# A hybrid encoder layer: 42 instead of 32 of 256 tokens served by gathered expert rows

## The chip, the cores and the metric

The kernel runs on one core of a Trainium2 chip. The metric is the device time of one execution in microseconds, the median of three runs. The core has a matrix engine (PE, with its weight loads listed apart as PEld), a vector engine (DVE), an activation engine (ACT), GpSimd (POOL), a queue engine that only issues transfers (SP), and 16 DMA engines.

## The reference

One encoder layer over 256 tokens of width 2048: a combined input projection, windowed attention, a state-space branch, a gated merge, and then PEER, in which the change lies. Cut to that part:

```
def peer(h, w_query, sub_keys_1, sub_keys_2, expert_down, expert_up):
    q = (ht @ w_query).reshape(t_, PEER_HEADS, 2, PEER_HALF)
    s1 = einsum('thd,hkd->thk', q[:, :, 0], sub_keys_1)
    s2 = einsum('thd,hkd->thk', q[:, :, 1], sub_keys_2)
    v1, i1 = top_k(s1, 16);  v2, i2 = top_k(s2, 16)
    ...
    top_s, pos = top_k(cand, 16)             # 8 heads x 16 = 128 experts for each token
    gate = softmax(top_s)
    ...
    u_sel = take(expert_down, ib)            # 16384 experts of width 2048
    act = einsum('tkd,td->tk', u_sel, hb)
    w = gb * gelu(act)
    v_sel = take(expert_up, ib)
    return einsum('tk,tkd->td', w, v_sel)
```

## The kernel before, in words

Up to the query projection of PEER the layer works through dense products; that part is not touched. For PEER the 256 tokens are divided. The first `NGT` = 32 tokens have their 128 expert rows fetched one by one from memory (**gathered**). The other `ND` = 224 tokens are computed **densely**: every one of the 16,384 experts is multiplied with every one of the 224 tokens, and a gate matrix (zero where an expert was not chosen) selects.

**The down stage** (lines 1299 to 1335) has 256 steps. A step takes half of a chunk of 128 experts: a 512 KB block `raw` is loaded on SP's queue into one of four buffers, ACT rounds it to `whi`, DVE subtracts the two to `wlo` (two buffers each), and PE issues 8 *high* products (line 1324: `whi` against the high and the low part of the tokens side by side, 2 x 224 = 448 columns) and 8 *low* ones (line 1331: `wlo` against the high part, 224 columns). After every second step `add` and `gelu` make the chunk's activations. **The up stage** (lines 1384 to 1464) has twice 128 steps (h = 0 and 1) of the same make: `raw`, `whi`, `wlo`, then 8 high products with the activations `wt` (high and low part, 448 columns, line 1415) and 8 low ones (224 columns, line 1418). For h = 1 two of the eight outputs are kept in a shared bank, and their high product is issued as two of 224 columns (lines 1412 and 1413).

Beside the steps run pieces of other work, put in by credits: at each step `pump` and `pump_bg` add a budget to a counter, and a generator is advanced until the counter is used up. Each `yield` names the cost of the piece before it, and `yield None` ends the pump's turn at this step. The order of each engine's instructions is fixed by this when the program is built (`pin`).

- `route` (line 1035), paced by `RB` = 1.2 a step: the sixteen best keys and experts for each head, mostly on DVE. It starts with the down stage. Its first piece, `scores`, goes through PE and ACT over some steps, and the first `top8` on DVE needs its result `sS`.
- `gates` (line 1129), paced by `GB` = 1.12, follows `route`: for four tokens at a time DVE makes one-hot rows `oh`, PE multiplies them (line 1154), and DVE or ACT puts the result `ax` into the activations `A0` and `A1` (`onto`).
- `gather` (line 1173), in the background queue `bg`, paced by `HB` = 0.42 a step in the down stage and `UB` = 0.55 in the up stage: `SG` = 4 slots of 32 tokens stand side by side on `PU` = 128 partitions, so that one indirect transfer on POOL's queue brings half rows (4 KB) of 128 experts, and `NGG` = 32 groups times two halves cover the 128 experts of each token. 64 times DVE forms a product and its sum (line 1219, cost 1.25) for the down table; then come a gelu and 64 times a scaled addition (line 146, into `last`, cost 1.2) for the up table. The up rows can start only when the down stage is over. `fold` then adds the slots up.
- `flips` (line 1371), after `gather` in the same queue: transposes and writes the first half of the output during h = 1.

Of the kernel before, what the change touches and what calls it, by code (L numbers as in the profile page):

```python
# [17 lines left out]
OP = mybir.AluOpType  # L18
AX = mybir.AxisListType

P = 128
# [22 lines left out]
GB = 1.12  # L44


NGT = 32
SG = 4
NGG = -(-128 // SG)
PU = SG * NGT  # L50
ND = T - NGT
HB = 0.42
LAND = 4
UB = 0.55


def _prep(x, mix_norm_g, w_in, q_norm_g, k_norm_g, attn_sink, w_attn_o,
# [54 lines left out]
def _layer(ctx: ExitStack, tc: tile.TileContext, a, out):  # L112
# [20 lines left out]
    def ax_ps():  # L133
        return psx.tile([P, 512], F32, name="ax", tag="ax")

    def tt(o, i0, i1, op, eng=None):
        return (eng or V).tensor_tensor(o, i0, i1, op=op)  # L137

    def ts(o, i0, s1, op0, s2=None, op1=None, eng=None):
        if op1 is None:  # L140
            (eng or V).tensor_scalar(o, i0, s1, None, op0=op0)  # L141
        else:
            (eng or V).tensor_scalar(o, i0, s1, s2, op0=op0, op1=op1)

    def stt(o, i0, s, i1, op0, op1, **kw):
        V.scalar_tensor_tensor(o, i0, s, i1, op0=op0, op1=op1, **kw)  # L146
# [4 lines left out]
    def copy(o, i, **kw):  # L151
        S.activation(o, i, AF.Copy, **kw)  # L152

    def f32(ap):
        return ap.bitcast(F32)
# [30 lines left out]
    for i2 in range(2):  # L186
        for q in range(2):
            p0 = i2 * 64 + q * 32
# [753 lines left out]
    iota = rt.tile([P, P], F32, name="iota")  # L942
# [6 lines left out]
    picks = rt.tile([P, 3, T], F32, name="picks")  # L949
# [14 lines left out]
    def top8(src, val, idx, scr=None):  # L964
        V.max(val, src)
        V.max_index(idx, val, src)
        if scr is not None:
            V.match_replace(out=scr, in_to_replace=val, in_values=src, imm_value=NEG)
# [21 lines left out]
    def slots():  # L990

        fl = rp.tile([P, 2, SG * NGG], F32, name="slf")
        ix = rp.tile([P, 2, SG * NGG], I32, name="sli")
        V.memset(fl, 0.0)
        tn = slice(0, NGT)
        stt(fl[tn, 0, 0:P], sel[0][tn, 0, :], float(NK), sel[0][tn, 1, :], OP.mult, OP.add)
        V.tensor_copy(fl[tn, 1, 0:P], sel[0][tn, 2, :])
        for h in range(2):
            ts(ix[tn, h], fl[tn, 0], 2.0, OP.mult, float(h), OP.add)
        for s_ in range(SG):  # L1000
            ps, gs = slice(s_ * NGT, (s_ + 1) * NGT), slice(s_ * NGG, (s_ + 1) * NGG)
            nc.gpsimd.dma_start(rix[ps], ix[tn, :, gs])
# [24 lines left out]
    state = {"half": 0}  # L1027

    def onward(gen):

        if moved[0] == state["half"]:
            yield None
        moved[0] = state["half"]
        next(gen, None)

    def route():
        items = [(b, cc) for b in range(NB) for cc in range(4)]
        first = scores(*items[0])
        while not scored:
            yield from onward(first)  # L1040
        for n, (b, cc) in enumerate(items):
            ahead = scores(*items[n + 1]) if n + 1 < len(items) else iter(())
            sS = scored.pop(0)
            val = rp.tile([P, 4, TOPK], F32, name="val", tag="val", bufs=2)
            idx = rp.tile([P, 4, TOPK], U32, name="idx", tag="idx", bufs=2)
            scr = rp.tile([P, P], F32, name="scr", tag="scr", bufs=2)
            for j in range(4):
                top8(sS[:, j, :], val[:, j, 0:8], idx[:, j, 0:8], scr)
                top8(scr, val[:, j, 8:16], idx[:, j, 8:16])
                yield 1.2  # L1050
                yield from onward(ahead)
            idf = rp.tile([P, 4, TOPK], F32, name="idf", tag="idf", bufs=2)
            V.tensor_copy(idf, idx)
            tops = rp.tile([P, 2, TOPK], F32, name="tops", tag="tops", bufs=2)
            pos = rp.tile([P, 2, TOPK], U32, name="pos", tag="pos", bufs=2)
            cand = rp.tile([P, TOPK, TOPK], F32, name="cand", tag="cand", bufs=2)
            cnd2 = rp.tile([P, TOPK * TOPK], F32, name="cnd2", tag="cnd2", bufs=2)
            for h in range(2):
                tt(cand, val[:, 2 * h, :].unsqueeze(2).to_broadcast([P, TOPK, TOPK]),
                   val[:, 2 * h + 1, :].unsqueeze(1).to_broadcast([P, TOPK, TOPK]), OP.add)  # L1060
                top8(cand.rearrange("p a b -> p (a b)"), tops[:, h, 0:8], pos[:, h, 0:8], cnd2)
                yield 1.5
                top8(cnd2, tops[:, h, 8:16], pos[:, h, 8:16])
                yield 0.75
            h0 = cc * 2 * TOPK
            gv = sel[b][:, 2, h0:h0 + 2 * TOPK].rearrange("p (h k) -> p h k", h=2)
            tt(gv, tops, tops[:, :, 0:1].to_broadcast([P, 2, TOPK]), OP.subtract)
            ab = rp.tile([P, 2, 2, TOPK], U32, name="ab", tag="ab", bufs=2)
            abf = rp.tile([P, 2, 2, TOPK], F32, name="abf", tag="abf", bufs=2)
            ts(ab[:, 0], pos, 4, OP.logical_shift_right)  # L1070
            ts(ab[:, 1], pos, 15, OP.bitwise_and)
            V.tensor_copy(abf.rearrange("p a h k -> p (a h k)"), ab.rearrange("p a h k -> p (a h k)"))
            yield 0.4
            eq = rp.tile([P, 2 * TOPK, TOPK], F32, name="eq", tag="eq", bufs=2)
            for w in range(2):
                tt(eq, abf[:, w].rearrange("p h k -> p (h k)").unsqueeze(2).to_broadcast(
                    [P, 2 * TOPK, TOPK]), iota16.unsqueeze(1).to_broadcast([P, 2 * TOPK, TOPK]),
                   OP.is_equal)
                for h in range(2):
                    e_ = eq[:, h * TOPK:(h + 1) * TOPK, :]  # L1080
                    tt(e_, e_, idf[:, 2 * h + w, :].unsqueeze(1).to_broadcast([P, TOPK, TOPK]), OP.mult)
                yield 1.25
                V.tensor_reduce(sel[b][:, w, h0:h0 + 2 * TOPK], eq, axis=AX.X, op=OP.add)
                yield 0.6
            while len(scored) == 0 and n + 1 < len(items):
                yield from onward(ahead)
            if cc == 3:
                yield from finish(b)
# [4 lines left out]
    def scaled():  # L1093
# [8 lines left out]
        for k in range(KD):  # L1102
            hs = rp.tile([P, ND], F32, name="hs", tag="hs", bufs=2)
            tt(hs, f32(xsh[:, k, NGT:]), f32(xsl[:, k, NGT:]), OP.add)
            tt(hs, hs, R[:, NGT:], OP.mult)
            copy(h2[:, k, 0, :], hs)
# [22 lines left out]
    def gates():  # L1129

        made, summed = [], []

        def onto():
            p0, gp = summed.pop(0)
            gv = gp.rearrange("p (t c) -> p t c", t=4)
            n = state["chunk"]
            for tile_, base, nch in ((A0, 0, CA), (A1, CA, NK - CA)):
                m = min(max(n - base, 0), nch)
                av = tile_[:, :, p0:p0 + 4].rearrange("p c t -> p t c")
                if m > 0:  # L1140
                    tt(av[:, :, :m], av[:, :, :m], gv[:, :, base:base + m], OP.mult)
                if m < nch:
                    copy(av[:, :, m:], gv[:, :, base + m:base + nch])
            state["tok"] = p0 + 4

        for t0 in range(0, ND + 8, 4):
            if summed:
                onto()
                yield 1.3
            if made:  # L1150
                p0, oh = made.pop(0)
                gp = ax_ps()
                for j in range(4):
                    PE.matmul(gp[:, j * P:(j + 1) * P], lhsT=oh[:, 0, j], rhs=oh[:, 1, j],
                              start=True, stop=True)
                summed.append((p0, gp))
            if t0 < ND:
                oh = rt.tile([P, 2, 4, P], F32, name="oh", tag="oh", bufs=2)
                tk = slice(NGT + t0, NGT + t0 + 4)
                tt(oh, iota.unsqueeze(1).unsqueeze(1).to_broadcast([P, 2, 4, P]),  # L1160
                   picks[:, 0:2, tk].unsqueeze(3).to_broadcast([P, 2, 4, P]), OP.is_equal)
                yield 1.15
                tt(oh[:, 1], oh[:, 1], picks[:, 2, tk].unsqueeze(2).to_broadcast([P, 4, P]), OP.mult)
                made.append((t0, oh))
                yield 0.6
            else:
                yield None

# [3 lines left out]
    def gather():  # L1172
# [6 lines left out]

        for s_ in range(SG):  # L1180
            ps = slice(s_ * NGT, (s_ + 1) * NGT)
# [119 lines left out]
    for s_ in range(2 * NK):  # L1301
        c, q = divmod(s_, 2)
# [9 lines left out]
        pump(RB if A1 is None else GB)  # L1312
        pump_bg(HB)
        nxt.append(next(ready))
# [67 lines left out]
    for h in range(2):  # L1382
# [11 lines left out]
        for c in range(NK):  # L1394
# [4 lines left out]
            if more:  # L1399
                nxt = [next(ready)]  # L1400
                gate_high((c + 1) % NK)
            pump_bg(UB)
            if more:
# [64 lines left out]
```

## Time and profile before

| | |
|---|---|
| median of 3 runs | 2305.19 us (2304.98 to 2305.86) |
| the profiled execution, its own time | 2304.5 us |
| its span, first to last instruction | 2302.7 us |
| busy, PE | 2238.8 us (97%) |
| busy, DVE | 1831.2 us (80%) |
| busy, ACT | 1217.9 us (53%) |
| mean DMA rate over the span | 225 GB/s |
| down stage | from 909.6 us to 1635 us |
| up stage | from 1637.7 us to the end |

The profile shows one execution. Busy times are per engine and overlap; a busy engine far from the end of a chain costs nothing. The times of the program's stages are those of the first and the last of their instructions in the timeline.

### The profile page before, as it was taken

How to read it: one execution, taken by the hardware profiler on the slowest of the kernel's cores; microseconds unless marked ns; L12 is line 12 of the kernel's file. 1: busy time of each engine (PE TensorE's matmuls, PEld its weight loads, DVE VectorE, ACT ScalarE, POOL GpSimd, SP SyncE). 2: the span in 40 equal slices, each digit the busy share in tenths (PEclk: the TensorE clock that was granted, in tenths of full speed). 3: DMA queues.
4: the chain of work that ended last, by engine and by line, in shares of the span. 5: the costliest groups of instructions: out<-in, count | busy, mean ns of one | idle time of the engine just before them, and what ended most of it. 6: DMA issues, size and time to landing. Idle time of an engine off the chain costs nothing. (4 is left out here: it accounts for less than half of the span.)

```text
span 2302.7 us, 36932 instructions
## 1 busy us (share of the span) xinstructions
PE 2238.8 (97%) x13298; PEld 1995.9 (87%) x13298; DVE 1831.2 (80%) x3819; ACT 1217.9 (53%) x2090; POOL 314.2 (14%) x309
## 2 busy tenths in 40 slices
PE   8999899999999999999999999999999999999999
PEld 6788676678888888898989999999999999999998
DVE  7858999974566565999989999999778878875565
ACT  5885654334344554455555555555555555554554
POOL 3320000001000100000012222112223322210000
PEclk9999999999999999999999999999999999999999
DMA  7854345566666765565577777777889888876664
GB/s 240 269 181 137 128 135 167 175 220 200 220 208 201 239 214 190 170 195 184 194 247 256 250 240 247 249 247 246 293 292 320 303 307 307 294 254 229 204 209 156
DMA packets 145464, 519.03 MB, mean 225 GB/s; under 512 B 18032, under 2 KB 18656, under 8 KB 144896
## 3 DMA queue, kind: packets, MB, share of 16 engines
q1 hardware_dynamic: 113184, 410.04, 53.2%
q0 software_dynamic: 30944, 105.56, 13.1%
q8 instruction: 104, 1.70, 0.3%
q10 hardware_dynamic: 1152, 1.07, 0.1%
q14 instruction: 80, 0.66, 0.1%
HBM read 496.11 MB, written 18.87 MB: 224 GB/s over the span
## 5 line engine op out<-in xcount | busy, mean ns | idle before, releaser
L152 ACT ACTIVATE whi<-raw 128x1024 fp32r<-128x1024 f32 x768 | 814.5, 1061 | 929.5 <-PE mm L286 227.5
L137 DVE TENSOR_TENSOR wlo<-raw,whi 128x1024 fp32r<-128x1024 f32 x768 | 939.1, 1223 | 389.9 <-ACT whi L152 372.7
L1324 PE MATMUL mm<-h,whi 128*128 128x448 f32 x2048 | 479.4, 370 | 0.1
L1324 PEld LDWEIGHTS mm<-h,whi 128*128 128x128 f32 x2048 | 367.3, 189 | 23.2 <-ACT whi L152 0.6
L1331 PEld LDWEIGHTS mm<-h,wlo 128*128 128x128 f32 x2048 | 265.9, 191 | 25.6 <-DVE wlo L137 18.5
L1331 PE MATMUL mm<-h,wlo 128*128 128x224 f32 x2048 | 271.3, 275 | 9.2 <-DVE wlo L137 8.6
L1415 PE MATMUL mm<-wt,whi 128*128 128x448 f32 x1024 | 252.2, 367 | 3.7 <-DVE wt L137 3.7
L285 PE MATMUL mm<-whi,hb 128*128 128x512 f32 x512 | 204.2, 401 | 7.7 <-DVE hb L141 6.4
L286 PE MATMUL mm<-whi,hb 128*128 128x512 f32 x512 | 202.8, 398 | 0.3 <-DVE hb L146 0.2
L1415 PE MATMUL ax<-wt,whi 128*128 128x448 f32 x768 | 198.1, 365 | 0.0
L1415 PEld LDWEIGHTS mm<-wt,whi 128*128 128x128 f32 x1024 | 174.5, 190 | 14.9 <-issue 3.3
L1204 POOL DMA_INDIRECT rows<-in_down_rows_dram,rix x64 | 108.8, 1700 | 394.5 <-DVE dots L1219 378.0
L289 PE MATMUL mm<-wlo,hb 128*128 128x512 f32 x512 | 148.3, 407 | 10.2 <-DVE wlo L137 10.0
L1418 PE MATMUL ax<-wt,wlo 128*128 128x224 f32 x1024 | 156.8, 275 | 0.0
L1418 PE MATMUL mm<-wt,wlo 128*128 128x224 f32 x1024 | 156.5, 275 | 0.0
L1415 PEld LDWEIGHTS ax<-wt,whi 128*128 128x128 f32 x768 | 144.1, 188 | 10.3
L1418 PEld LDWEIGHTS mm<-wt,wlo 128*128 128x128 f32 x1024 | 144.9, 191 | 3.9
L1418 PEld LDWEIGHTS ax<-wt,wlo 128*128 128x128 f32 x1024 | 135.8, 193 | 0.0
L289 PEld LDWEIGHTS mm<-wlo,hb 128*128 128x128 f32 x512 | 92.9, 189 | 44.4 <-DVE wlo L137 26.4
L285 PEld LDWEIGHTS mm<-whi,hb 128*128 128x128 f32 x512 | 97.0, 190 | 30.2 <-ACT whi L152 10.2
L286 PEld LDWEIGHTS mm<-whi,hb 128*128 128x128 f32 x512 | 96.9, 190 | 20.1 <-DVE hb L146 1.1
L137 DVE TENSOR_TENSOR X<-X,s 128x64 f32<-128x64 f32 x508 | 107.9, 282 | 0.0
(276 smaller groups left out, 3190.2 us busy)
## 6 DMA issues: line engine op xcount, KB each, us to landing
raw<-in_down_dram SPq DMA_DIRECT2D x256, 512.0 KB, 4.2
raw<-in_up_dram SPq DMA_DIRECT2D x256, 512.0 KB, 4.8
raw<-in_w_in_dram SPq DMA_DIRECT2D x128, 512.0 KB, 3.6
raw<-in_w_ao_dram SPq DMA_DIRECT2D x32, 512.0 KB, 3.9
raw<-in_w_out_dram SPq DMA_DIRECT2D x32, 512.0 KB, 4.0
raw<-in_w_q_dram SPq DMA_DIRECT2D x32, 512.0 KB, 4.5
raw<-in_wgb_dram SPq DMA_DIRECT2D x16, 512.0 KB, 4.4
raw<-in_wga_dram SPq DMA_DIRECT2D x16, 512.0 KB, 3.7
```

What stands on the lines that cost most here:

```text
L137: return (eng or V).tensor_tensor(o, i0, i1, op=op)
L152: S.activation(o, i, AF.Copy, **kw)
L285: PE.matmul(ps[b], lhsT=lh[:, k, bs], rhs=h_, start=(k == 0), stop=False)
L286: PE.matmul(ps[b], lhsT=ll[:, k, bs], rhs=h_, start=False, stop=False)
L289: PE.matmul(ps[b], lhsT=lh[:, k, b * P:(b + 1) * P], rhs=lo[:, j * 512:(j + 1) * 512], start=False, stop=(k == 2 * nu - 1))
L1204: nc.gpsimd.indirect_dma_start(out=r[:PU], out_offset=None, in_=table, in_offset=bass.IndirectOffsetOnAxis(ap=rix[:PU, h, g:g + 1], axis=0))
L1324: PE.matmul(ps[:, :2 * ND], lhsT=hi[:, j * P:(j + 1) * P], rhs=h2[:, k].rearrange("p a t -> p (a t)"), start=(k == 0), stop=(k == KD - 1), ...
L1331: PE.matmul(ps[:, :ND], lhsT=lo[:, j * P:(j + 1) * P], rhs=h2[:, q * 8 + j, 0, :], start=False, stop=False, skip_group_check=True)
L1415: PE.matmul(acc[i][:, :2 * ND], lhsT=w_, rhs=wv, start=first, stop=False, skip_group_check=True)
L1418: PE.matmul(region(i)[0], lhsT=lo[:, i * P:(i + 1) * P], rhs=wh, start=False, stop=end, skip_group_check=True)
```

## The change

Three constants say how many tokens are gathered: 42 in three slots (126 partitions, 43 groups of experts, 86 transfers for each table) in place of 32 in four; 214 tokens remain dense. The background's pace is 0.40 a step in the down stage and 0.66 in the up stage. `route` gives up two further turns between its first scores and the first `top8`; `gates` gives up one after its first one-hot rows, and takes a last group of two tokens, since 214 is not a multiple of four.

```
-NGT = 32
-SG = 4
+NGT = 42
+SG = 3
 NGG = -(-128 // SG)
 PU = SG * NGT
 ND = T - NGT
-HB = 0.42
+HB = 0.4
 LAND = 4
-UB = 0.55
+UB = 0.66
...
         while not scored:
             yield from onward(first)
+        yield None
+        yield None
...
         for t0 in range(0, ND + 8, 4):
             if summed:
                 onto()
                 yield 1.3
             if made:
-                p0, oh = made.pop(0)
+                p0, nt, oh = made.pop(0)
                 gp = ax_ps()
-                for j in range(4):
+                for j in range(nt):
                     PE.matmul(gp[:, j * P:(j + 1) * P], lhsT=oh[:, 0, j], rhs=oh[:, 1, j],
                               start=True, stop=True)
-                summed.append((p0, gp))
+                summed.append((p0, nt, gp))
             if t0 < ND:
+                nt = min(4, ND - t0)
...
                 yield 0.6
+                if t0 == 0:
+                    yield None
             else:
                 yield None
```

In what is left out, slices of four tokens become slices of `nt`.

How the instructions move is shown at three places. First, DVE at the start of `route` in the down stage: `wlo` is the step's own subtraction, `ge` the sum before the activation, and `MAX` the first `top8` on the scores `sS`. Before:

```order
L137 TENSOR_TENSOR wlo<-raw,whi 128x1024 x16
L137 TENSOR_TENSOR ge<-ge,mm 128x224
L965 MAX val<-sS 128x8
L966 MAX_INDEX idx<-val,sS 128x8
L968 MATCH_REPLACE scr<-val,sS 128x128
```

Now:

```order
L137 TENSOR_TENSOR wlo<-raw,whi 128x1024 x16
L137 TENSOR_TENSOR ge<-ge,mm 128x214
L137 TENSOR_TENSOR wlo<-raw,whi 128x1024 x2
L137 TENSOR_TENSOR ge<-ge,mm 128x214
L965 MAX val<-sS 128x8
L966 MAX_INDEX idx<-val,sS 128x8
L968 MATCH_REPLACE scr<-val,sS 128x128
```

The first `top8` stands two steps later, behind two more `wlo` and one more `ge`.

Second, PE at the start of `gates`: `ax<-oh` are the products of the one-hot rows, between the step's high (`whi`) and low (`wlo`) products. Before:

```order
L1331 MATMUL mm<-h_7619,wlo 128x224 x8
L1324 MATMUL mm<-h_7619,whi 128x448
L1154 MATMUL ax<-oh 128x128 x4
L1324 MATMUL mm<-h_7619,whi 128x448 x7
L1331 MATMUL mm<-h_7619,wlo 128x224 x8
L1324 MATMUL mm<-h_7619,whi 128x448
L1154 MATMUL ax<-oh 128x128 x4
```

Now:

```order
L1336 MATMUL mm<-h_7619,wlo 128x214 x8
L1329 MATMUL mm<-h_7619,whi 128x428 x8
L1336 MATMUL mm<-h_7619,wlo 128x214 x8
L1329 MATMUL mm<-h_7619,whi 128x428
L1156 MATMUL ax<-oh 128x128 x8
L1329 MATMUL mm<-h_7619,whi 128x428 x7
L1336 MATMUL mm<-h_7619,wlo 128x214 x8
```

The first group is issued together with the second, a step later than its one-hot rows, and the step's products have 428 and 214 columns.

Third, DVE at the end of `gather` in the up stage: `last<-...,wg,last` is a scaled addition of gathered rows, `wt` the step's own subtraction on the activations, `fold` what follows the last row, and `last<-last,ax` the first of the four pieces of `flips`. Before:

```order
L146 SCALAR_TENSOR_TENSOR last<-rows_11110,wg,last 128x1024
L137 TENSOR_TENSOR wlo<-raw,whi 128x1024
L137 TENSOR_TENSOR wt<-A_8155,wt 128x224
L137 TENSOR_TENSOR wlo<-raw,whi 128x1024
L137 TENSOR_TENSOR wt<-A_8155,wt 128x224
L137 TENSOR_TENSOR fold<-ident 128x32
L137 TENSOR_TENSOR fold<-fold,ident 128x32 x2
```

Now:

```order
L146 SCALAR_TENSOR_TENSOR last<-h2t,wg,last 126x1024
L137 TENSOR_TENSOR wlo<-raw,whi 128x1024
L137 TENSOR_TENSOR wt<-A_11137,wt 128x214
L137 TENSOR_TENSOR wlo<-raw,whi 128x1024
L137 TENSOR_TENSOR wt<-A_11137,wt 128x214
L137 TENSOR_TENSOR fold<-ident 128x42
L137 TENSOR_TENSOR fold<-fold,ident 128x42
```

The same pieces stand at a later step: counted by `wlo` over both stages, 512 in all, the last scaled addition moves from step 423 to step 484 and the last piece of `flips(0)` from 431 to 491. Of the products for the down table 52 of 64 were issued before the up stage, and now 49 of 86.

## Rows read from the trace of the kernel before

**Rows 1.** The page: busy time, and granted clock and GB/s in 40 slices

```profile
PE 2238.8 (97%) x13298; PEld 1995.9 (87%) x13298; DVE 1831.2 (80%) x3819; ACT 1217.9 (53%) x2090; POOL 314.2 (14%) x309
...
PEclk9999999999999999999999999999999999999999
...
GB/s 240 269 181 137 128 135 167 175 220 200 220 208 201 239 214 190 170 195 184 194 247 256 250 240 247 249 247 246 293 292 320 303 307 307 294 254 229 204 209 156
```

**Rows 2.** Windows: stretch, length, busy of PE PEld DVE ACT POOL, clock, DMA, GB/s

```profile
909.60:1158.20 248.60, 239.52 (x1506) 220.50 (x1505) 234.09 (x635) 129.02 (x195) 4.15 (x8) 0.99 0.57 185
1158.20:1593.20 435.00, 432.68 (x2868) 412.67 (x2867) 411.20 (x604) 231.65 (x452) 90.98 (x60) 1.00 0.73 248
1593.20:1637.70 44.50, 42.33 (x274) 39.98 (x273) 36.41 (x55) 23.70 (x43) 10.51 (x10) 1.00 0.81 271
...
1665.00:1960.00 295.00, 294.76 (x1878) 280.65 (x1877) 235.90 (x296) 157.31 (x238) 87.17 (x54) 1.00 0.88 306
```

**Rows 3.** Timeline of PE: start, time, products of 512, 448 and 224 columns

```profile
906.74 0.39 PE L286 MATMUL mm<-whi,xs 128*128 128x512 f32 x1
...
908.10 0.39 PE L286 MATMUL mm<-whi,xs 128*128 128x512 f32 x1
...
1505.08 1.79 PE L1324 MATMUL mm<-h,whi 128*128 128x448 f32 x8
1506.70 1.05 PE L1331 MATMUL mm<-h,wlo 128*128 128x224 f32 x8
1507.59 1.82 PE L1324 MATMUL mm<-h,whi 128*128 128x448 f32 x8
```

**Rows 4.** Groups by form: weight loads of 128, 64 and 32 columns

```profile
L1418 PEld LDWEIGHTS mm<-wt,wlo 128*128 128x128 f32 x1024 | 144.9, 191 | 3.9
...
L697 PEld LDWEIGHTS ax<-X,ccl 128*64 128x64 f32 x256 | 21.4, 136 | 2.6 <-issue 1.1
...
L1358 PEld LDWEIGHTS ax<-last,fold 128*32 128x32 f32 x6 | 0.4, 108 | 0.5 <-issue 0.5
```

**Rows 5.** Groups by form, costliest first: ACT and DVE in the steps

```profile
L137 DVE TENSOR_TENSOR wlo<-raw,whi 128x1024 fp32r<-128x1024 f32 x410 | 501.7, 1224 | 200.3 <-ACT whi L152 199.4
L152 ACT ACTIVATE whi<-raw 128x1024 fp32r<-128x1024 f32 x409 | 434.1, 1061 | 497.5 <-PE ax L1413 157.9 <-PE ax L1415 146.0 <-PE mm L1324 82.2
...
L1219 DVE CUSTOM_DVE_ANT_0 rows<-rows,h2t 128x1024 f32<-128x1024 f32 x64 | 78.0, 1220 | 0.0
...
L146 DVE SCALAR_TENSOR_TENSOR last<-rows,wg,last 128x1024 f32<-128x1024 f32 x37 | 47.4, 1280 | 0.0
```

**Rows 6.** Waits, longest first: us in total, times, longest

```profile
PEld mm L1331 <- DVE wlo L137: 18.5, 29, 4.3
```

**Rows 7.** Timeline of DVE, PEld and PE: `route`'s and `gates`' first waits

```profile
919.88 0.29 DVE L965 MAX8 val<-sS 128x8 f32<-128x128 f32 x1 [2.37 <-ACT sS L152]
922.73 0.97 PEld L1331 LDWEIGHTS mm<-h,wlo 128*128 128x128 f32 x8 [0.45 <-DVE wlo L137]
1179.06 1.16 PE L1154 MATMUL ax<-oh 128*128 128x128 f32 x8 [2.11 <-DVE oh L137]
```

**Rows 8.** Timeline of the up stage, DVE and PE, with gathered rows in it

```profile
1899.04 1.23 DVE L137 TENSOR_TENSOR wlo<-raw,whi 128x1024 fp32r<-128x1024 f32 x1 [0.86 <-ACT whi L152]
...
1901.69 1.22 DVE L137 TENSOR_TENSOR wlo<-raw,whi 128x1024 fp32r<-128x1024 f32 x1
...
1903.66 0.98 PE L1415 MATMUL mm<-wt,whi 128*128 128x448 f32 x4
...
1905.21 0.39 DVE L137 TENSOR_TENSOR wt<-A,wt 128x224 fp32r<-128x224 f32 x1
...
1906.18 0.98 PE L1415 MATMUL mm<-wt,whi 128*128 128x448 f32 x4
```

**Rows 9.** DMA issues: size and median time from issue to landing

```profile
raw<-in_up_dram SPq DMA_DIRECT2D x256, 512.0 KB, 4.8
...
rows<-in_up_rows_dram,rix POOLq DMA_INDIRECT x38, 7.6
```

More of the change, by code (lines that the diff above doesn't have):

```diff
@@ L44 @@
 GB = 1.12
-NGT = 32
-SG = 4
+NGT = 42
+SG = 3
 NGG = -(-128 // SG)
@@ L51 @@
 ND = T - NGT
-HB = 0.42
+HB = 0.4
 LAND = 4
-UB = 0.55
+UB = 0.66
 def _prep(x, mix_norm_g, w_in, q_norm_g, k_norm_g, attn_sink, w_attn_o,
@@ L1040, in route @@
             yield from onward(first)
+        yield None
+        yield None
         for n, (b, cc) in enumerate(items):
@@ L1133, in onto @@
         def onto():
-            p0, gp = summed.pop(0)
-            gv = gp.rearrange("p (t c) -> p t c", t=4)
+            p0, nt, gp = summed.pop(0)
+            gv = gp.rearrange("p (t c) -> p t c", t=4)[:, :nt]
             n = state["chunk"]
@@ L1138, in onto @@
                 m = min(max(n - base, 0), nch)
-                av = tile_[:, :, p0:p0 + 4].rearrange("p c t -> p t c")
+                av = tile_[:, :, p0:p0 + nt].rearrange("p c t -> p t c")
                 if m > 0:
@@ L1143, in onto @@
                     copy(av[:, :, m:], gv[:, :, base + m:base + nch])
-            state["tok"] = p0 + 4
+            state["tok"] = p0 + nt
         for t0 in range(0, ND + 8, 4):
@@ L1150, in gates @@
             if made:
-                p0, oh = made.pop(0)
+                p0, nt, oh = made.pop(0)
                 gp = ax_ps()
-                for j in range(4):
+                for j in range(nt):
                     PE.matmul(gp[:, j * P:(j + 1) * P], lhsT=oh[:, 0, j], rhs=oh[:, 1, j],
                               start=True, stop=True)
-                summed.append((p0, gp))
+                summed.append((p0, nt, gp))
             if t0 < ND:
+                nt = min(4, ND - t0)
                 oh = rt.tile([P, 2, 4, P], F32, name="oh", tag="oh", bufs=2)
-                tk = slice(NGT + t0, NGT + t0 + 4)
-                tt(oh, iota.unsqueeze(1).unsqueeze(1).to_broadcast([P, 2, 4, P]),
-                   picks[:, 0:2, tk].unsqueeze(3).to_broadcast([P, 2, 4, P]), OP.is_equal)
+                tk = slice(NGT + t0, NGT + t0 + nt)
+                tt(oh[:, :, :nt], iota.unsqueeze(1).unsqueeze(1).to_broadcast([P, 2, nt, P]),
+                   picks[:, 0:2, tk].unsqueeze(3).to_broadcast([P, 2, nt, P]), OP.is_equal)
                 yield 1.15
-                tt(oh[:, 1], oh[:, 1], picks[:, 2, tk].unsqueeze(2).to_broadcast([P, 4, P]), OP.mult)
-                made.append((t0, oh))
+                tt(oh[:, 1, :nt], oh[:, 1, :nt], picks[:, 2, tk].unsqueeze(2).to_broadcast([P, nt, P]), OP.mult)
+                made.append((t0, nt, oh))
                 yield 0.6
+                if t0 == 0:
+                    yield None
             else:
```

## The prediction

> **What bounds the kernel now.** I read the page's busy times first, then its granted clock, then windows cut at the stages that the change touches, then the timeline of PE inside a step. [...] By stages [rows 2]: while `route` runs (909.6 to 1158.2 us, 88 steps) DVE is busy 234.1 of 248.6 us, and PE's low weight loads wait 18.5 us in total for DVE's `wlo` [rows 6], so this stretch belongs to DVE more than to PE. While `gates` and `gather` run together (1158.2 to 1593.2 us, 152 steps) PE is busy 432.7 of 435.0 us and DVE 411.2: PE bounds it, with DVE at 95%. In the up stage (1665 to 1960 us) PE is busy 294.8 of 295.0 us, DVE only 80%, but the DMA engines 88%. So fewer columns on PE should shorten the second and the third stretch in full and the first in part.
>
> **The high products.** They lose 20 of 448 columns. What a column costs comes from the starts in the timeline [rows 3]: six products of 512 columns take 908.10 - 906.74 = 1.36 us, 226.7 ns each; eight of 448 take 1506.70 - 1505.08 = 1.62 us, 202.5 ns each. The slope is 24.2/64 = 0.378 ns a column, which makes 7.6 ns for 20; scaling 202.5 ns by 20/448 makes 9.0. I take 8.0. There are 256 x 8 in the down stage, 128 x 8 for h = 0 and 128 x 6 for h = 1: 3840 x 8.0 ns = 30.7 us, of which 5.6 lie in `route`'s 88 steps, 9.7 in the next 152, 1.0 in the last 16 and 14.3 in the up stage.
>
> **The low products.** They lose 10 of 224 columns, 4608 of them (8 in each of 512 steps, and 4 split high ones for h = 1). Eight take 1507.59 - 1506.70 = 0.89 us, 111 ns each [rows 3]. The same slope would take off up to 4.2 ns. But each of them also loads 128 columns of weights: a load lasts 191 ns with 128 columns, 136 with 64 and 108 with 32 [rows 4], 83/96 = 0.86 ns a column, so 128 columns need about 111 ns of loading whatever follows. That is the interval itself. I take 0, with 4.2 ns x 4608 = 19.4 us as the other end; 0 is nearer, because the two numbers coincide.
>
> **Gate products.** Ten tokens fewer, each two records that I price like a low product, 111 ns: 2.2 us of PE.
>
> **What DVE gives back.** In `route` DVE's work a step stays the same, so of the 5.6 us I take half, 2.8; the ends are 0 and 5.6. In the next 152 steps DVE needs 411.2/152 = 2.71 us a step against PE's 2.86. The change takes 0.02 x 1.22/1.25 = 0.02 us a step from the background [rows 5], so DVE needs 2.69 against 2.80 for PE. It still fits on average, but at 96%, and the pieces are lumpy: I take 8.5 of 9.7, ends 5 and 9.7.
>
> **The 44 added row operations.** 22 products of 1.22 us and 22 additions of 1.28 us [rows 5], 55 us of DVE. Nearly all goes to the up stage, where 37 of the 86 products are now issued. There 0.66/1.2 = 0.55 rows a step take the place of 0.458, 0.12 us of DVE more; a step lasted 1906.18 - 1903.66 = 2.52 us [rows 8] and should last 2.46; DVE's 235.9/295.0 x 2.52 = 2.02 us becomes 2.14 of it. Where a step with a row follows another (20 such pairs by the order), `wlo`, `wt` and the row take 1901.69 - 1899.04 = 2.65 us, 0.19 us longer than a step; two make 0.38, and `wt` now ends at 1905.60, 0.58 us ahead of its product at 1906.18 [rows 8]. So they are covered. I price them at nothing; if the cover went, a pair would cost at most 0.38 us, 8 us in all. The end of `gather` and `flips(0)` moves to step 491 of 512, so 20 steps, some 50 us, are left, and the tail is what it was.
>
> **The transfers.** A step of the up stage loads 0.524 MB of `raw` and before 0.458 x 0.524 MB of rows, 0.764 MB; now 0.55 x 0.516 MB, 0.808 MB, in 2.46 instead of 2.52 us: 1.083 times the rate. The share of 0.88 at 306 GB/s [rows 2] becomes 0.95 at 331 GB/s, for about 230 of the 256 steps instead of 168. No row shows that rate. A `raw` load has four steps less `whi` and `wlo` to land, 4 x 2.46 - 1.06 - 1.22 = 7.6 us [rows 5], and lands in 4.8 at the median; gathered rows take 7.6 [rows 9]. Some loads will come late. The ends are 0 and the whole 14.3 us of this stage; I take 3, nearer to 0 because PE loses 0.2 us in 295 at a share of 0.88.
>
> **The first waits.** DVE no longer waits 2.37 us for `sS`, but the two steps that it now gives up cost it as much; PE's own stop behind it, 0.45 us and a smaller one, goes. The first gate product's wait of 2.11 us goes too [rows 7], since its one-hot rows are ready by the next step. Together 2.5 us; ends 0 and 4.8 (both waits in full and a little more).
>
> **Sum.** 2.8 + 8.5 + 1.0 + 14.3 + 0 + 2.2 + 2.5 - 3 = 28.3 us less. The profiled execution took 2304.5 us, 0.7 below the median of 2305.19, so its own sum is 2276.2 and I predict **2276**.
>
> **The rivals.**
>
> *The low products shorten too.* For it: 111 ns also fits a straight line from 448 columns, 202.5 - 224 x 0.41. Against it: the weight loads' 111 ns. All of the up stage's 2560 x 4.2 = 10.7 us and about half of the down stage's 8.6 would come on top: 2261. [...] Chance 0.20.
>
> *DVE bounds the down stage.* If its bursts leave nothing of the 2.8 and the 8.5 us, the time is 2287.5. For it: DVE at 95% before. Against it: PE lost 2.3 us in 435. Chance 0.10.
>
> *The DMA engines eat the up stage's gain.* If they deliver no more than the 320 GB/s of the best slice [rows 1], a step of 0.808 MB stays at 2.52 us and the other 11 us of the gain are lost: 2287. Rows of 126 partitions need not spread evenly over 16 engines; the gathered part of the share is 0.95 x 0.284/0.808 = 0.33, so an engine with 0.38/0.33 = 1.15 times its part would be busy all the time. Chance 0.10.
>
> [...]
>
> *Slower: `raw` paces the up stage.* The same place, but the engines deliver no more than on average before. At 306 GB/s a step of 0.808 MB takes 2.64 us, 0.18 more than PE's, over 230 steps 41 us, against the 28.3 + 3 gained otherwise: 2314. It turns to slower when less than about 309 GB/s is delivered, and to no change up to 313. Against it: the slice with 320 GB/s [rows 1] lies in a stretch in which PE did not stop. Chance 0.04, and 0.03 for ending near no change.
>
> That the change does not do what it says is excluded by the order: the columns are 428 and 214, and the row work does end in time.
>
> **How the numbers follow.** Forecast 0.53, the low products 0.20, DVE 0.10, DMA 0.10, no change 0.03, slower 0.04. The range reaches from 2258 (the low products, and half the late loads I priced) to 2291 (DVE or DMA taking their part). About 0.2% is what a measurement can tell from no change, 2300.6 to 2309.8 us: faster 0.93, same 0.03, slower 0.04.
>
> **What would show it.** In the changed profile: high products at 194 to 195 ns from start to start and low ones still at 110 to 111; PE's waits for `wlo` during `route` as long as before or longer; the first `oh` wait gone; in the up stage a DMA share near 0.95, with `raw` landing in more than 6 us and only a few microseconds of PE idle. The prediction is wrong if low products start 107 ns apart, if ACT waits for `raw` by tens of microseconds, or if the high products' intervals fall by less than 7 ns.

## The result and the profile after

The changed kernel took **2385.98 us** (median of 4 runs, 2382.97 to 2393.67) against 2305.24 us of the kernel before: a ratio of 1.0352 [1.0339, 1.0366], 3.5% slower, where 2276 us and "faster" were forecast. The profiled execution took 2387.56 us, its span is 2385.8 us.

The page of the changed kernel, beside [rows 1]: busy times, DMA share and rate in 40 slices, the two DMA queues (packets, MB, their time as a share of the span of 16 engines), and the chain that ended last.

```profile
PE 2248.3 (94%) x13278; PEld 2009.9 (84%) x13278; DVE 1872.7 (78%) x3872; ACT 1215.8 (51%) x2087; POOL 361.8 (15%) x349
...
DMA  6853335557666665555687877789999999999975
GB/s 234 267 175 130 133 133 185 172 187 239 210 214 214 216 209 175 194 187 192 211 263 252 253 242 252 241 262 283 269 276 273 269 272 277 272 278 268 268 234 182
...
q1 hardware_dynamic: 113184, 410.04, 54.8%
q0 software_dynamic: 39936, 127.24, 19.3%
...
PE 53%; DVE 16%; DMA 12%; issue 2%; ACT 2%; POOL 0%; DVEq 0%; ACTq 0%
DMA raw<-in_up_dram 12%; PE mm L1329 11%; DVE wlo L137 7%; PE mm L1336 7%; PE mm L1420 5%; PE mm L289 5%; PE mm L286 5%; PE mm L285 5%; PE ax L1420 3%; PE mm L1423 2%; PE ax L1423 2%; DVE X L137 2%; DVE s L137 2%; PE ax L1156 2%; ACT whi L152 2%
```

The same two lines of the page of the kernel before:

```profile
DMA  7854345566666765565577777777889888876664
...
q0 software_dynamic: 30944, 105.56, 13.1%
```

Three things stand out. `raw` of the up stage is 12% of the chain, some 286 us. The DMA digits read 9 over nearly the whole up stage, and the rate under them is about 270 GB/s, where the kernel before reached 292 to 320 GB/s in slices that read 8 or 9 [rows 1]. And q0, the gathers' queue, took 19.3% of 2385.8 us for 127.24 MB, 3.62 us of 16 engines for one MB. In the kernel before it took 13.1% of 2302.7 us for 105.56 MB, 2.86 us. Some 38 MB of q0 are not gathers (105.56 less 128 transfers of 0.524 MB), so for the gathers alone the difference is larger than these figures say; further down it is read in the up stage only.

The windows, cut as in [rows 2] at the stages' own borders (us, busy of PE, PEld, DVE, ACT, POOL with counts, clock, DMA share, GB/s):

```profile
913.70:1158.70 245.00, 235.50 (x1507) 220.47 (x1506) 230.08 (x622) 128.64 (x195) 3.56 (x6) 0.99 0.56 187
1158.70:1587.00 428.30, 424.30 (x2864) 413.36 (x2862) 409.86 (x605) 233.16 (x456) 82.86 (x55) 1.00 0.80 248
1587.00:1628.60 41.60, 39.48 (x260) 38.41 (x258) 31.60 (x49) 22.72 (x37) 10.56 (x10) 1.00 0.93 278
1628.60:2300.00 671.40, 594.08 (x3824) 566.16 (x3825) 483.28 (x623) 303.78 (x463) 174.15 (x121) 0.99 1.01 272
```

All three stretches of the down stage became shorter (248.6, 435.0 and 44.5 us before). The loss lies in the last row alone: PE stands still for 77 of 671 us while the DMA engines are full (as this row shows, the share can read a little over 1). From its first product to the end the up stage took 757.2 us (1628.6 to 2385.8) against 665.0 (1637.7 to 2302.7): 92.2 us more. What is waited for there, in the view of waits (total us, times, longest), beside [rows 6]:

```profile
ACT whi L152 <- DMA raw<-in_up_dram: 209.8, 104, 4.0
PEld mm L1420 <- DVE wt L137: 92.9, 86, 2.4
...
PE mm L1420 <- DVE wt L137: 79.0, 78, 2.2
...
PEld mm L1336 <- DVE wlo L137: 22.9, 35, 3.2
```

Before, ACT waited once for `raw` of the up stage, 1.4 us. One such stall, in the timeline of ACT, DVE and PE (start, time, instruction, in brackets the idle time before it):

```profile
1645.55 1.06 ACT L152 ACTIVATE whi<-raw 128x1024 fp32r<-128x1024 f32 x1 [2.53 <-DMA raw<-in_up_dram]
...
1646.64 1.23 DVE L137 TENSOR_TENSOR wlo<-raw,whi 128x1024 fp32r<-128x1024 f32 x1 [2.34 <-ACT whi L152]
1647.79 0.38 DVE L137 TENSOR_TENSOR wt<-A,wt 128x214 fp32r<-128x214 f32 x1
...
1648.21 1.04 PE L1420 MATMUL mm<-wt,whi 128*128 128x428 f32 x4 [1.17 <-DVE wt L137]
```

`raw` lands late, `whi` and `wlo` follow at once, `wt` stands behind `wlo` on DVE, and PE's next high product waits for `wt`. So here PE's wait for `wt` is a wait for `raw`, three links on. Over the whole kernel PE waited 3.7 us for `wt` before and 79.0 us now, and in the version with 128 rows below 4.7 us. The gathered rows of that stage now take a median of 11.1 us to land (the view of DMA issues), against 7.6 [rows 9]:

```profile
rows<-in_up_rows_dram,rix POOLq DMA_INDIRECT x51, 11.1
```

PE's timeline shows what the columns brought, beside [rows 3], and the first gate products, beside [rows 7]:

```profile
1183.06 1.73 PE L1329 MATMUL mm<-h,whi 128*128 128x428 f32 x8
1184.63 1.04 PE L1336 MATMUL mm<-h,wlo 128*128 128x214 f32 x8
1185.51 0.37 PE L1329 MATMUL mm<-h,whi 128*128 128x428 f32 x1
1185.72 1.05 PE L1156 MATMUL ax<-oh 128*128 128x128 f32 x8
1188.58 1.16 PE L1156 MATMUL ax<-oh 128*128 128x128 f32 x8 [1.81 <-DVE oh L137]
```

Eight high products take 1184.63 - 1183.06 = 1.57 us, 196 ns each (202.5 before); eight low ones 0.88 us, 110 ns (111 before). The first group of gate products no longer waits. The second one does, 1.81 us, where the first waited 2.11.

### The profile page after: what moved, and what is told of

It is laid out like the page before. It is cut to its first block, busy times and chain, and to the rows that moved or that the text cites. A ratio compares the mean times of both kernels' runs of the same rounds, so it can differ in the third digit from the quotient of the medians.

```text
span 2385.8 us, 37053 instructions
## 1 busy us (share of the span) xinstructions
PE 2248.3 (94%) x13278; PEld 2009.9 (84%) x13278; DVE 1872.7 (78%) x3872; ACT 1215.8 (51%) x2087; POOL 361.8 (15%) x349
## 2 busy tenths in 40 slices
DMA packets 154457, 540.72 MB, mean 227 GB/s; under 512 B 21718, under 2 KB 22362, under 8 KB 153890
## 3 DMA queue, kind: packets, MB, share of 16 engines
q0 software_dynamic: 39936, 127.24, 19.3%
## 4 chain that ended last, share of the span: by engine, by line
PE 53%; DVE 16%; DMA 12%; issue 2%; ACT 2%; POOL 0%; DVEq 0%; ACTq 0%
DMA raw<-in_up_dram 12%; PE mm L1329 11%; DVE wlo L137 7%; PE mm L1336 7%; PE mm L1420 5%; PE mm L289 5%; PE mm L286 5%; PE mm L285 5%; PE ax L1420 3%; PE mm L1423 2%; PE ax L1423 2%; DVE X L137 2%; DVE s L137 2%; PE ax L1156 2%; ACT whi L152 2%
## 5 line engine op out<-in xcount | busy, mean ns | idle before, releaser
L1329 PE MATMUL mm<-h,whi 128*128 128x428 f32 x2048 | 463.7, 363 | 0.4 <-ACT whi L152 0.4
L1420 PE MATMUL mm<-wt,whi 128*128 128x428 f32 x1024 | 257.2, 372 | 79.4 <-DVE wt L137 79.0
L1336 PE MATMUL mm<-h,wlo 128*128 128x214 f32 x2048 | 271.8, 276 | 11.3 <-DVE wlo L137 10.8
L1209 POOL DMA_INDIRECT rows<-in_down_rows_dram,rix x86 | 137.1, 1594 | 486.1 <-DVE dots L1224 462.3
L1420 PE MATMUL ax<-wt,whi 128*128 128x428 f32 x768 | 192.8, 359 | 0.0
L1423 PE MATMUL ax<-wt,wlo 128*128 128x214 f32 x1024 | 158.3, 277 | 0.0
L1423 PE MATMUL mm<-wt,wlo 128*128 128x214 f32 x1024 | 156.9, 275 | 0.0
```

The source lines that it names most:

```text
L1209: nc.gpsimd.indirect_dma_start(out=r[:PU], out_offset=None, in_=table, in_offset=bass.IndirectOffsetOnAxis(ap=rix[:PU, h, g:g + 1], axis=0))
L1329: PE.matmul(ps[:, :2 * ND], lhsT=hi[:, j * P:(j + 1) * P], rhs=h2[:, k].rearrange("p a t -> p (a t)"), start=(k == 0), stop=(k == KD - 1), ...
L1336: PE.matmul(ps[:, :ND], lhsT=lo[:, j * P:(j + 1) * P], rhs=h2[:, q * 8 + j, 0, :], start=False, stop=False, skip_group_check=True)
L1420: PE.matmul(acc[i][:, :2 * ND], lhsT=w_, rhs=wv, start=first, stop=False, skip_group_check=True)
L1423: PE.matmul(region(i)[0], lhsT=lo[:, i * P:(i + 1) * P], rhs=wh, start=False, stop=end, skip_group_check=True)
```

## The experiments

A ratio is that to the kernel before, run beside each version, with its 95% interval. After the result two theories stood. **A, the form:** gathers into 126 partitions are carried worse than gathers into 128, and this lowers what the DMA engines deliver for everything. **B, the pace:** 0.55 gathered rows a step beside a shorter step are more than the engines deliver in any form.

### The change with gathers of 128 rows

The two partitions that have no expert get row 0 of the table as filler; the row work stays on 126.

```
+        nc.gpsimd.memset(rix.bitcast(F32).rearrange("p h g -> p (h g)"), 0.0)
...
-                        out=r[:PU], out_offset=None, in_=table,
-                        in_offset=bass.IndirectOffsetOnAxis(ap=rix[:PU, h, g:g + 1], axis=0))
+                        out=r, out_offset=None, in_=table,
+                        in_offset=bass.IndirectOffsetOnAxis(ap=rix[:, h, g:g + 1], axis=0))
```

> The change as it is, but each gather brings 128 rows to 128 partitions instead of 126 to 126; the two added partitions fetch row 0 of the table and are used by nothing. Theory A (form): the 126-partition transfers themselves are carried badly by the DMA engines, so with 128 the 4 KB packets go at the pace of the kernel before, the up stage's DMA share is 0.95 or less, ACT's wait for raw falls from 210 us to under 20, and the time is 2270 to 2285. Theory B (pace): 0.55 rows a step beside the raw loads is more than the DMA engines carry, whatever the form; then the time stays at 2375 to 2395, since 1.6% more bytes are moved.

Measured: 2284.22 us (2279.09 to 2286.27), ratio 0.9898 [0.9881, 0.9914]. Two more partitions, 1.1% more bytes in q0, and the kernel is 102 us faster than the changed one. The middle of its up stage in the windows; below it the same stretch of the changed kernel:

```profile
1665.00:2200.00 535.00, 532.38 (x3619) 521.38 (x3617) 452.32 (x581) 286.64 (x437) 181.66 (x113) 1.00 0.91 322
```

```profile
1665.00:2200.00 535.00, 473.29 (x3032) 451.21 (x3031) 385.62 (x500) 243.63 (x373) 142.36 (x99) 0.99 1.02 273
```

The engines deliver 322 GB/s at a share of 0.91, or 354 GB/s for a full share; with 126 partitions it is 273/1.02 = 268. ACT's wait for `raw` falls from 209.8 to 23.9 us, a little over the 20 that theory A allowed. In the view of DMA issues of the version with 128, the rows land in 8.1 us at the median instead of 11.1, and `raw` in 6.3, within the 7.6 us that the prediction gives a load:

```profile
raw<-in_up_dram SPq DMA_DIRECT2D x256, 512.0 KB, 6.3
...
rows<-in_up_rows_dram,rix POOLq DMA_INDIRECT x51, 8.1
```

The form explains the loss. With 128 rows the pace is carried.

### The kernel before with 126 partitions, and with the faster pace

The other direction: the form alone, and the pace alone, each in the kernel before.

```
-PU = SG * NGT
+PU = SG * NGT - 2
```

> The kernel before with its gathers cut to 126 of 128 partitions, pace and all else as it was; it leaves out experts 96 to 127 of tokens 30 and 31. Theory A (form): its up stage slows as the change's did; at 0.458 rows a step the load is less, so 2320 to 2370, with ACT waiting for raw by 20 to 100 us. Theory B (pace): fewer bytes at the old pace, so 2304 to 2306.

```
-UB = 0.55
+UB = 0.66
```

> The kernel before with the up stage's background pace at 0.66 instead of 0.55, 128 partitions, 0.55 rows a step, so the gather is done in fewer steps. Theory A (form): the engines carry this pace, 2303 to 2309, DMA share about 0.93 while rows are gathered. Theory B (pace): the up stage slows while it gathers, as in the change 0.35 us a step over some 140 steps, so 2340 to 2360.

Measured: 126 partitions, 2342.17 us (2340.8 to 2345.0), ratio 1.0153 [1.0136, 1.017]; the faster pace, 2306.37 us, ratio 0.9998 [0.9988, 1.0008]. In the windows, first the kernel with 126 partitions, then the one with the pace:

```profile
1665.00:1960.00 295.00, 277.48 (x1708) 259.56 (x1708) 216.66 (x272) 144.24 (x216) 75.96 (x49) 0.99 0.97 276
```

```profile
1665.00:1960.00 295.00, 294.28 (x1868) 279.73 (x1868) 246.14 (x304) 156.71 (x235) 104.06 (x65) 1.00 0.92 322
```

Leaving two of 128 partitions out costs 1.5%, with fewer bytes than before; ACT waits 99.3 us for `raw`, against 1.4. The pace costs nothing: 322 GB/s are delivered at 0.92 and PE does not stop. So A is shown from both sides, and B falls.

### What about 126 is it: other counts of partitions

Two theories of the cause. **E, the even count:** gathers into a count of partitions that 16 divides are carried as well as those into 128, so 126 and 120 are slow, and 112, 96 and 64 are not. **P, the partitions:** anything short of all 128 is carried badly beside loads of 128 partitions. The kernel before, with `PU` smaller by 8, 16, 32 and 64:

```
-PU = SG * NGT
+PU = SG * NGT - 16
```

> The kernel before with its gathers cut to 112 of 128 partitions; it leaves out experts 96 to 127 of tokens 16 to 31. [...]

> The kernel before with its gathers cut to 120 of 128 partitions; it leaves out experts 96 to 127 of tokens 24 to 31. [...]

> The kernel before with its gathers cut to 96 of 128 partitions; it leaves out experts 96 to 127 of all gathered tokens. [...] Theory P (place): over 0.135% per MB; with a quarter fewer bytes the time shows less of it, 2305 to 2330.

> The kernel before with its gathers cut to 64 of 128 partitions; it leaves out experts 64 to 127 of all gathered tokens. With half the bytes the time says little (2303 to 2312). Read by queue q0's share of the engines per MB: 0.124 to 0.128% if a transfer that 16 divides into groups of four partitions is carried well, which would leave 112 and 96 (seven and six) as the bad ones; over 0.135% if anything short of 128 partitions is carried badly beside the 128-partition loads.

Measured: 112 partitions 2313.49 us, ratio 1.0026 [1.0011, 1.0042]; 120: 2337.08, 1.0132 [1.0112, 1.0152]; 96: 2311.88, 1.0027 [1.0016, 1.0037]; 64: 2304.4 us in one run. Each has fewer bytes to move than the kernel before, and yet the intervals of 112, 120 and 96 are clear of 1. By time 96 falls in P's range, but the two counts that 16 divides lose only 0.3% where 120 loses 1.3%, and 64 cannot tell, so the queues have to decide. The windows of 112, 96 and 64 partitions, in this order:

```profile
1665.00:1960.00 295.00, 291.64 (x1836) 275.88 (x1835) 230.21 (x290) 153.50 (x231) 95.83 (x53) 1.00 0.97 285
```

```profile
1665.00:1960.00 295.00, 292.14 (x1849) 276.98 (x1848) 231.32 (x291) 155.00 (x232) 101.29 (x54) 1.00 0.95 277
```

```profile
1665.00:1960.00 295.00, 294.79 (x1877) 280.55 (x1876) 235.29 (x296) 157.27 (x237) 103.12 (x54) 1.00 0.89 257
```

With 64 partitions the gathers bring half the bytes, 257 instead of 306 GB/s, and fill the same share, 0.89 against 0.88 [rows 2]. The queues of all kernels in the up stage, from the view of DMA for 1665 to 1960 us (of the changed kernel and its variant with 128 rows, 1665 to 2200). q0 and q1 stand in us of 16 engines for one MB, the queue's share times the window over its MB; in this window q0 carries gathers and q1 the `raw` loads. "For a full share" is GB/s over share. The lines of the kernel before, and then of the one with 64 partitions, from which the first and the last row are worked out:

```profile
q1 hardware_dynamic: 16886, 61.50, 61.4%
q0 software_dynamic: 7776, 28.32, 25.8%
```

```profile
q1 hardware_dynamic: 16866, 61.42, 71.2%
q0 software_dynamic: 4320, 14.16, 17.4%
```

| gathers | q0, us for one MB | q1, us for one MB | GB/s, DMA share | for a full share |
|---|---|---|---|---|
| 128 partitions, before | 2.69 | 2.95 | 306, 0.88 | 348 |
| 128 partitions, before, faster pace | 2.70 | 2.92 | 322, 0.92 | 350 |
| 128, the change | 2.74 | 2.89 | 322, 0.91 | 354 |
| 126, the change | 4.04 | 3.55 | 273, 1.02 | 268 |
| 126, before | 3.79 | 3.37 | 276, 0.97 | 285 |
| 120, before | 4.06 | 3.38 | 274, 0.98 | 280 |
| 112, before | 3.68 | 3.29 | 285, 0.97 | 294 |
| 96, before | 3.68 | 3.33 | 277, 0.95 | 292 |
| 64, before | 3.63 | 3.42 | 257, 0.89 | 289 |

The counts that 16 divides (112, 96, 64) cost 3.63 to 3.68 us for one MB, 35 to 37% more than 128, and nearly as much as 126 in the same kernel. In the terms of the expectations, q0's share of the span on the profile's page for one MB, 112 comes to 0.144% and 96 to 0.146%, over P's 0.135, where the kernel before has 0.124%. E as the main cause falls; P stands. The `raw` loads on q1 cost 12 to 16% more for one MB too: the short gathers slow the loads beside them. That 112 partitions lose only some 6 us (by the ratio) does not speak for E: a step then needs 0.524 + 0.458 x 0.459 = 0.734 MB in 2.52 us, 291 GB/s, just what the engines deliver for a full share (294), while a step with 126 needs 302, and there they deliver 285.

With 126 and 120 the engines deliver some 10 GB/s less for a full share than with 112 (285 and 280 against 294), and that may come with a count that 16 does not divide. An estimate of its part: at the costs with 112 partitions the changed step of 0.524 MB on q1 and 0.284 MB on q0 would take 0.524 x 3.29 + 0.284 x 3.68 = 2.77 us, 0.31 more than the 2.46 forecast, 71 us over some 230 steps. The change lost 103 us, so about a third could come from the count. No run separates the two, and the estimate takes it that the costs of one MB carry over.

The small packets differ with the count. The view of DMA of the changed kernel, and then of the version with 128 rows:

```profile
DMA packets 154457, 540.72 MB, mean 227 GB/s; under 512 B 21718, under 2 KB 22362, under 8 KB 153890
```

```profile
DMA packets 151705, 542.11 MB, mean 237 GB/s; under 512 B 18622, under 2 KB 19266, under 8 KB 151138
```

The 172 gathers of 126 rows have 21718 - 18622 = 3096 packets under 512 B more, 18 each. Over the 128 gathers of the kernel before, 126 partitions add 18 each (20336 against 18032), 120 add 8 each (19056), and 112 and 96 add none (18033 and 18032). So the counts that 16 does not divide bring small packets that these two do not, but this is not what the short counts have in common. What these packets are, and why short gathers cost more, is not shown: the traces here do not name the engine of a packet, and no run has short gathers without full loads beside them.

### The three added yields

The version with 128 rows, without the two turns that `route` gives up and the one of `gates`.

```
         while not scored:
             yield from onward(first)
-        yield None
-        yield None
...
                 yield 0.6
-                if t0 == 0:
-                    yield None
```

> The 128-partition version without the three yields that move the first waits back. If the yields are worth the 2.5 us that the prediction gave them, it is 2 to 3 us slower than the 128-partition version with them; if the waits only moved (the changed profile still shows a 2.08 us stop at the second group of gate products), within 1 us of it.

Measured: 2283.79 us, ratio 0.9899 [0.9882, 0.9915], against 0.9898 [0.9881, 0.9914] with them. The two versions are within 1 us, so the waits only moved. The yields are worth nothing that can be measured.

### Four microseconds before PEER begins

The changed kernel starts its down stage at 913.7 us, the kernel before at 909.6, though no instruction ahead of it was changed. What differs is memory: `A0`'s slot has 78 x 214 = 16692 numbers instead of 74 x 224 = 16576, and the tiles behind it lie 464 bytes further on. First the version with 128 rows, with that slot rounded up to a multiple of 64 numbers; then the kernel before with only the slot made 16692 numbers.

```
-    A0 = pp.tile([P, CA, ND], F32, name="A0", tag="X")
+    A0 = pp.tile([P, -(-CA * ND // 64) * 64], F32, name="A0", tag="X")[:, :CA * ND].rearrange("p (c t) -> p c t", c=CA)
```

> The 128-partition version with the slot of A0 rounded up to a multiple of 64 numbers (16704 instead of 16692), so that the tiles behind it lie 512 bytes further on than in the kernel before and not 464. Theory (placement): the dense products whose weights come from such a tile (hb and mb) took 234 ns from start to start where they took 227 before, because of that place; they return to 227, the first product of the down stage starts at 909 to 911 us instead of 913.8, and the time falls by 2 to 5 us against the 128-partition version. Rival (chance of the execution): nothing changes, 2282 to 2286.

```
-    A0 = pp.tile([P, CA, ND], F32, name="A0", tag="X")
+    A0 = pp.tile([P, 16692], F32, name="A0", tag="X")[:, :CA * ND].rearrange("p (c t) -> p c t", c=CA)
```

> The kernel before with nothing changed but the slot of A0: 16692 numbers as in the change instead of 16576, so that the tiles behind it lie 464 bytes further on. Theory (placement): the dense products with weights from hb and mb take 234 ns from start to start instead of 227, the first product of the down stage starts at 912 to 915 us instead of 909.6, and the time is 2308 to 2313. Rival (chance of the execution): 2304 to 2307 with 227 ns.

Measured, for the rounded slot: 2277.73 us (2276.17 to 2280.27), ratio 0.9876 [0.986, 0.9893], its down stage from 909.3 us: the fastest version of all. For the shifted slot in the kernel before: 2312.41 us, ratio 1.0024 [1.0014, 1.0033], its down stage from 914.6 us. The gain of the rounded slot, 6.5 us, is more than the 2 to 5 expected; its interval overlaps that of the version without it, [0.9881, 0.9914], so what shows the cause is the shifted slot, whose interval is clear of 1, and the timelines. The groups by line of the kernel before and then of the one with the shift (total busy, mean ns; idle before):

```profile
L1415 PE MATMUL mm<-wt,whi 128*128 128x448 f32 x1024 | 252.2, 367 | 3.7 <-DVE wt L137 3.7
L285 PE MATMUL mm<-whi,hb 128*128 128x512 f32 x512 | 204.2, 401 | 7.7 <-DVE hb L141 6.4 <-ACT whi L152 1.3
```

```profile
L1415 PE MATMUL mm<-wt,whi 128*128 128x448 f32 x1024 | 254.2, 369 | 3.7 <-DVE wt L137 3.7
L285 PE MATMUL mm<-whi,hb 128*128 128x512 f32 x512 | 206.6, 405 | 9.2 <-DVE hb L141 8.4 <-ACT whi L152 0.6
```

The products are the same, and each lasts 2 to 4 ns longer on average. In the timeline of the shifted kernel eight products of 512 columns with `mb` start in 1.86 us, 232.5 ns apart:

```profile
741.98 0.39 PE L285 MATMUL mm<-whi,mb 128*128 128x512 f32 x1
...
743.61 0.40 PE L286 MATMUL mm<-whi,mb 128*128 128x512 f32 x1
743.84 0.63 PE L289 MATMUL mm<-wlo,mb 128*128 128x512 f32 x2
```

In the version with the rounded slot they are 227 ns apart again, six in 1.36 us:

```profile
741.42 0.39 PE L285 MATMUL mm<-whi,mb 128*128 128x512 f32 x1
...
742.78 0.39 PE L285 MATMUL mm<-whi,mb 128*128 128x512 f32 x1
```

So where a product's tile starts in memory matters here, 232.5 ns against 227 from start to start, and the change lost 4 us by that before its first step. The shift costs later too: in the kernel before it lengthens the up stage by 2.6 us (2311.4 - 1643.8 against 665.0). Which tile, and which starts are good ones, is not shown; only two shifts, of 464 and 512 bytes, were tried.

## Why the prediction was wrong

The forecast, 28.3 us less, set against the spans of the changed kernel and of the best version, stage by stage:

| us against before | predicted | the change | 128 rows, rounded slot |
|---|---|---|---|
| ahead of the down stage | 0 | +4.1 | -0.3 |
| down stage | -17.0 | -13.2 | -13.6 |
| up stage | -11.3 | +92.2 | -12.8 |
| span | -28.3 | +83.1 | -26.7 |

**The step that failed is "The transfers".** It took the gathers of 126 partitions to be carried like those of 128, put the rate at 331 GB/s and a share of 0.95, and priced late loads at 3 us with 14.3 as the far end. With 128 rows that holds: 322 GB/s at 0.91, and the up stage gains 10.5 us (665.0 - 654.5), or 12.8 with the rounded slot. With 126 the engines deliver 273 GB/s. The prediction's own arithmetic then gives 0.808 MB / 273 GB/s = 2.96 us a step instead of 2.46, over some 230 steps 115 us. Measured between the forms, 757.2 - 654.5 = 103 us. For 126 partitions in the kernel before, 0.76 MB / 276 GB/s = 2.75 us against 2.52 over 168 steps is 39 us; measured 31 to 39, by the ratio's interval.

**The rival that came true** is the fourth, `raw` paces the up stage. Its mechanism and its place were right, and its threshold of 309 GB/s lies between the 273 that was slower and the 322 that was not. Its price (2314 us, from 306 GB/s) and its chance (0.04) were not, since the rate of before was taken as the least that the engines deliver. Bounding the new form from the nearest rows failed there: every row came from 128 partitions, and none bounded a form of transfer that the trace did not contain. The stated range left it out: 2314 us lies above its upper end of 2291, and the far end of the term, 14.3 us, below the 41 us that this rival itself reckons. The rival beside it, that the engines eat the gain, had an uneven spread in view (1.15 times, its own estimate) but let it cost no more than the gain; how the rows are spread over the engines no run shows.

**The high products** were sized right. In the rows above they start 196 ns apart where 194 to 195 were forecast, 6 ns less than before and so, by those eight alone, under the 7 ns that the prediction named as a sign of being wrong. Over all neighbouring high products of the down stage, some 1720 in each trace, the median interval falls from 203 to 195 ns, the 8.0 that was taken. **The low products** stayed at 110 ns, as forecast: eight of them went from 111 to 110 ns, and over the neighbouring low products of the down stage, 1792 in each trace, the median interval from 112 to 111. The rival that they shorten too falls. Its 4.2 ns for 10 columns no run shows; the slope of 0.378 ns a column, which the prediction names for it, gives 3.8, and the runs showed 1. The gate products, with 128 columns and a load of 128 columns of weights each, also start 112 ns apart at the median, so between 128 and 224 columns the interval does not follow the columns. That fits the 111 ns of loading that the prediction estimated; more on what sets the interval is not shown.

**The down stage** gave 13.2 of 17.0 us. `route` gave 3.6 (2.8, and 0.4 of the first waits, forecast). The next 152 steps gave 6.7 instead of 8.5 and the gate wait's 2.1; DVE is busy 409.86 of 428.30 us there, the forecast 96%, and PE's idle time grew from 2.3 to 4.0 us. The last 16 steps and the gate products gave 2.9 of 3.2.

**The first waits** were a wrong term: 2.5 us were forecast, and without the yields the time is the same. The gate wait moved to the second group, 1.81 us instead of 2.11: DVE makes one-hot rows for the second group after the first, and PE, with both groups in hand at one step, waits for the later. That next wait was not looked for.

**The 44 row operations** were rightly priced at nothing, as far as the version with 128 rows shows: at 0.55 rows a step DVE is busy 452 of 535 us, and PE, which it could hold up, 532.

**Of the signs named**, "ACT waits for `raw` by tens of microseconds" came clearly: 209.8 us. With 128 rows it is 23.9, and with the rounded slot 20.3:

```profile
ACT whi L152 <- DMA raw<-in_up_dram: 20.3, 14, 2.2
```

That is what is left of the 3 us that were priced; its share of the end was not separated. The best version's 2277.73 us is 0.1% from the forecast, and part of that is luck: a down stage that gained less than forecast and an up stage that gained more offset each other.

One sum of the prediction does not come out: 2261 us less half of the 3 us of late loads is 2259.5, not 2258. It changes nothing here.

## What to carry to other kernels

Before the partition count of a stream of transfers is changed, ask what the trace shows of that form. Where it shows none, the bound is not the rate of the form that is there; here a stage with a DMA share of 0.88 had no room for the unknown form, and became 92.2 us longer. If the count of useful rows falls short of 128, try filler rows in the rest: 1% more bytes on the gathers' queue took away 102 us here. And when a size changes, look at where the tiles behind it begin, and compare the stages ahead of the change as well: in this case they differed by 4 us, and that was the sign.

## What the runs showed that was not expected

- Gathers into 126, 120, 112, 96 or 64 partitions, beside loads into 128, took 3.63 to 4.06 us of the 16 engines for one MB in the up stage, against 2.69 to 2.74 with 128. The engines' delivery for a full share fell from about 350 GB/s to between 268 and 294, and the full loads beside them slowed too. Why is not shown. Two gathers of 64 partitions side by side were not tried.
- Tiles moved by 464 bytes cost 0.24%: products of 512 columns with `mb` started 232.5 ns apart instead of 227. Those with `xs` in the same trace stayed at 227 ns:

```profile
906.05 0.39 PE L285 MATMUL mm<-whi,xs 128*128 128x512 f32 x1
...
907.41 0.39 PE L285 MATMUL mm<-whi,xs 128*128 128x512 f32 x1
```
